# Second layer of a two-layer trunk: the first attention pair's projections, scores and sums ahead of the value projection, its transposes and value products behind it

## The chip, the cores and the metric

The kernel runs on one core of a Trainium2 chip. The metric is the device time of one execution in microseconds; before the change three runs had a median of 1221.72 us (1219.8 to 1224.15). The engines of the core are named as in the profile: PE multiplies matrices (PEld is its weight load), ACT applies functions and casts, DVE does elementwise work and scans, POOL is hardly used, and SP issues most of the transfers. Each engine works through its own queue in the order of the program and waits there on semaphores of the others.

## The reference

`x` is 512 x 1024 in float32. Layer 0 is left alone by this change. Layer 1 projects `x`, runs a gated recurrence (C) on one half of the channels and stick-breaking attention (D, 8 heads of 64) on the other, joins them with an output projection and a residual, and ends in a feed-forward block:

```
proj = x @ od_w_in[o]
xr, gr, qd, kd, vd = split_cols(proj, [LRU_WIDTH, LRU_WIDTH, HALF, HALF, HALF])
yc = rg_lru_branch(xr, gr, ...)
yd = stick_breaking_attention(qd, kd, vd)
mix = jnp.concatenate([yc, yd], axis=-1) @ od_w_out[o]
...
z = jnp.einsum('bqhd,bkhd->bhqk', q[:, q0:q1], k[:, :q1]).astype(jnp.float32) * scale
log_one_minus = jnp.where(mask, jax.nn.log_sigmoid(-z), 0.0)
suffix = lax.cumsum(log_one_minus, axis=3, reverse=True) - log_one_minus
log_w = jax.nn.log_sigmoid(z) + suffix
w = jnp.where(mask, jnp.exp(log_w), 0.0)
outs.append(jnp.einsum('bhqk,bkhd->bqhd', w.astype(v.dtype), v[:, :q1]))
```

The values `vd` are wanted only by the last of these lines.

## The kernel before

Matrices are multiplied in three passes: each float32 operand is split into a high part (a cast on ACT, L241 for weights, L247 elsewhere) and a low part (a subtraction on DVE, L242 and L248), and PE adds up high x high (L252), and the two mixed products (L253, L254). A projection of 128 output channels (`proj`, tile `pj`) is 24 matmuls over 512 columns; a weight chunk arrives by an SP transfer (L234) into one of two buffers `ws` and is split into one of five buffers `wh`, `wl`.

In layer 1 `griffin` does the recurrence: four channel blocks on ACT and DVE (L858 to L907), with four gate projections on PE beside them, and the split of its four results (L247, L248: `yh`, `yl`). Then `values` makes the 512 x 512 value matrix with four blocks of 24 matmuls (tile `pv`, copied out at L289). Then four calls of `sb_pair`, each for two heads:

- `qk_pair` projects q and k (24 matmuls each). q's bank is evacuated by ACT L723 and DVE L726, for each of two heads in turn; k's by ACT L730 and L731 and DVE L732 (`kz`), again for each head. ACT and DVE take turns on a bank.
- Five tiles of scores `z` (L933, L934, the mask L935), each followed by ACT L937 to L939 and DVE L940, L943 (a running sum, backwards) and L944, which leaves log weights `l`.
- Each tile is transposed on PE (L951, bank `pt` or `po`) and goes through exp into `pT` (ACT L957).
- 16 matmuls with the values (L964, tile `po`), and the split of the result.

Projections and values share two banks of the tag "g" in turn, so each new block of 24 matmuls has to wait until the one before the last has been evacuated.

What stands behind what on an engine is not set by the code's order alone: a scheduler orders the instructions by a priority that follows the order of the code, with weight splits pulled ahead by 600 places (`self.hp`). While one pair's ACT and DVE work runs, PE is given the next pair's projections; beside the fourth pair it has the recurrence's rows of the output projection (`out_rows`, 96 matmuls).

Of the kernel before, what the change touches and what calls it, by code (L numbers as in the profile page):

```python
# [11 lines left out]
AF = mybir.ActivationFunctionType  # L12
# [3 lines left out]
P = 128  # L16
# [28 lines left out]
S_GR, S_QD, S_KD, S_VD, S_WO1 = S_XR + 4, S_XR + 8, S_XR + 12, S_XR + 16, S_XR + 20  # L45
# [11 lines left out]
class Trunk:  # L57
# [853 lines left out]
        return ys  # L911


    def sb_pair(self, hp, v):
        nc = self.nc
        A = nc.scalar.activation
        q, k = self.qk_pair(S_QD + hp, S_KD + hp, self.kz)
        yh, yl = self.act("yh"), self.act("yl")
        po = self.bank("ho", "po")


        tiles = (((0, 3, 0),), ((1, 3, 0),), ((0, 2, 0), (0, 0, 384)), ((1, 2, 0), (1, 0, 384)), ((0, 1, 0), (1, 1, 256)))
        pT = self.t2k("pT", [P, 20 * P], tag="pT")
        at = ((15, -6), (1, 5))
        rev = lambda a: a[:, ::-1]
        for ti, parts in enumerate(tiles):
            tag = "zl"[ti % 2]
            l = self.t2k("l", tag=tag)
            ps = self.bank(("s", "s", "sc")[ti % 3], "z")
            for e, i, o in parts:  # L930
                n = (i + 1) * P
                c = slice(i * P, n)
                nc.tensor.matmul(ps[:, o:o + n], q[e][:, c], k[e][:, 0:n], start=True, stop=False)  # L933
                nc.tensor.matmul(ps[:, o:o + n], q[e][:, c], self.kz[e][:, 0:n], start=False, stop=False)  # L934
                nc.tensor.matmul(ps[:, o + i * P:o + n], self.identb, self.sbmask, start=False, stop=True)  # L935

            A(l, ps, AF.Abs)  # L937
            A(l, l, AF.Exp, scale=-1.0)
            A(l, l, AF.Ln, bias=self.one)  # L939
            nc.vector.scalar_tensor_tensor(l, ps, 0.0, l, ALU.max, ALU.add)  # L940
            for e, i, o in parts:
                r = rev(l[:, o:o + (i + 1) * P])
                nc.vector.tensor_tensor_scan(r, self.ones1[:, 0:(i + 1) * P], r, 0.0, ALU.mult, ALU.add)  # L943
            nc.vector.tensor_tensor(l, ps, l, ALU.subtract)  # L944
            pt = self.bank(("pt", "po")[ti % 2], "pt")
            for e, i, o in parts:
                b, step = at[e]
                for j in range(i + 1):

                    m = j if step > 0 else i - j  # L950
                    nc.tensor.transpose(pt[:, o + m * P:o + (m + 1) * P], l[:, o + j * P:o + (j + 1) * P], self.ident)  # L951
            for e, i, o in parts:
                b, step = at[e]
                lo = b + i + (0 if step > 0 else i * step)
                dst = bass.AP(tensor=pT.tensor, offset=pT.offset + lo * P,
                              ap=[pT.ap[0], [abs(step) * P, i + 1], [1, P]])
                A(dst, pt[:, o:o + (i + 1) * P].rearrange("p (j t) -> p j t", t=P), AF.Exp)  # L957
        cp = self.newest()

        for j in range(NTB):  # L960
            for e in range(2):
                h = 2 * hp + e
                x = (at[e][0] + at[e][1] * j + j) * P
                nc.tensor.matmul(po[64 * e:64 * e + 64, j * P:T], v[j][:, h * 64:h * 64 + 64], pT[:, x:x + T - j * P],  # L964
                                 start=j == 0, stop=j == NTB - 1)
                if j == 0 and e == 0:
                    self.behind(self.newest(), cp)
        self.put(po, yh, yl)
        return yh, yl

    def layer1(self, xr):
        self.qk4 = False

        self.kz = [self.t2k("kz", dt=F32R, tag="kz") for _ in range(2)]
        for e in range(2):
            self.nc.gpsimd.memset(self.kz[e][64 - 64 * e:P - 64 * e].bitcast(F32), 0.0)
        self.ones1 = self.t2k("ones", tag="one")
        self.nc.gpsimd.memset(self.ones1, 1.0)
        yc = self.griffin(xr)
        self.hp = 600  # L980
        v = self.values(S_VD)
        self.hp = 600
        yd = []
        for hp in range(4):
            yd.append(self.sb_pair(hp, v))
            if hp == 3:
                self.out_rows(yc, S_WO1)
        self.hp = 1
        return yd
# [123 lines left out]
```

## Time and profile before

| | us |
|---|---|
| median of three runs | 1221.72 |
| the profiled execution, its own time | 1221.14 |
| its span in the trace | 1219.3 |
| DVE busy in the span | 757.4 |
| ACT busy in the span | 518.6 |
| transfers, mean rate over the span | 105 GB/s |

In the span's time layer 1's value blocks run from 701 us to 723 us, the first pair's q and k from 723 to 736, and the four pairs from 736 to about 826. The list of groups gives for a line of the program the count, the busy time and the mean of one; the timeline gives start and length of each instruction, and in brackets how long its engine had been idle and who released it. Matmul lengths overlap, so the pace of PE is read from start to start.

### The profile page before, as it was taken

The page shows a single profiled execution, that of the slowest core. Times are in us where ns is not written, and L with a number is a line of the kernel's source. Part 1 is how long each engine was busy: PE and PEld are TensorE (multiplying, and loading weights), DVE is VectorE, ACT ScalarE, POOL GpSimd, SP SyncE. Part 2 cuts the span into 40 slices and gives each one's busy share as a digit, 9 for nine tenths or more (in the row PEclk, how much of TensorE's full clock was granted, in tenths as well). Part 3 has the DMA queues.
Part 4 walks back from the last instruction along what each step waited for, and adds up shares of the span by engine and source line. Part 5 has one row for each costly group of instructions (what it writes and reads, how often), then busy time and mean ns, then how long its engine had stood idle before and what let it go on. Part 6 is the DMA issues. An engine that isn't in the chain of part 4 may idle for free.

```text
span 1219.3 us, 15337 instructions
## 1 busy us (share of the span) xinstructions
PE 1196.5 (98%) x6063; PEld 970.6 (80%) x6063; DVE 757.4 (62%) x1141; ACT 518.6 (43%) x790; POOL 55.8 (5%) x80
## 2 busy tenths in 40 slices
PE   9999999999999999999999998999999999999997
PEld 6787777778888888878889786677988888888886
DVE  7638798769355634554368876887753644456346
ACT  7447568443233423332233667872332433333220
POOL 1000000001001000200000000000000100010001
PEclk9999999999999999999999999999999999999999
DMA  6421211233637432643324222112644643464321
GB/s 244 150 75 53 87 44 50 65 122 99 230 92 121 134 104 87 106 132 108 91 82 156 68 74 83 35 35 87 199 164 93 115 139 91 100 104 138 104 69 69
DMA packets 38727, 127.96 MB, mean 105 GB/s; under 512 B 4592, under 2 KB 6128, under 8 KB 38656
## 3 DMA queue, kind: packets, MB, share of 16 engines
q1 hardware_dynamic: 32496, 108.44, 28.0%
q0 software_dynamic: 4864, 16.81, 8.3%
q10 hardware_dynamic: 1296, 1.73, 0.4%
q8 instruction: 48, 0.79, 0.3%
q14 instruction: 23, 0.19, 0.1%
HBM read 124.84 MB, written 2.10 MB: 104 GB/s over the span
## 4 chain that ended last, share of the span: by engine, by line
PE 88%; DVE 4%; ACT 3%; DMA 2%; issue 1%; SPq 0%; DVEq 0%; ACTq 0%
PE pf L253 13%; PE pf L252 13%; PE pf L254 13%; PE pj L252 4%; PE pj L253 4%; PE pj L254 4%; PE po L254 4%; PE po L253 4%; PE po L252 4%; PE fa L252 2%; PE fa L254 2%; PE fa L253 2%; PE pv L253 2%; PE pv L252 2%; PE pv L254 2%; DMA wwal<-in_wst 1%
## 5 line engine op out<-in xcount | busy, mean ns | idle before, releaser
L241 ACT CAST wh<-ws 128x1024 fp32r<-128x1024 f32 x143 | 150.2, 1051 | 304.9 <-PE pf L253 121.8
L242 DVE TENSOR_TENSOR wl<-ws,wh 128x1024 fp32r<-128x1024 f32 x143 | 174.8, 1223 | 153.5 <-ACT wh L241 149.9
L252 PE MATMUL pf<-xh,wh 128*128 128x512 f32 x640 | 249.0, 389 | 0.0
L253 PE MATMUL pf<-xl,wh 128*128 128x512 f32 x640 | 249.0, 389 | 0.0
L254 PE MATMUL pf<-xh,wl 128*128 128x512 f32 x640 | 249.0, 389 | 0.0
L254 PEld LDWEIGHTS pf<-xh,wl 128*128 128x128 f32 x640 | 120.2, 188 | 25.0
L253 PEld LDWEIGHTS pf<-xl,wh 128*128 128x128 f32 x640 | 120.2, 188 | 24.9
L252 PEld LDWEIGHTS pf<-xh,wh 128*128 128x128 f32 x640 | 120.2, 188 | 24.7
L527 DVE TENSOR_TENSOR s<-s,pf 128x512 f32<-128x512 f32 x44 | 30.3, 688 | 148.0 <-PE pf L254 148.0
L252 PE MATMUL pj<-xh,wh 128*128 128x512 f32 x256 | 104.2, 407 | 2.1 <-DVE qk L726 2.1
L254 PE MATMUL pj<-xh,wl 128*128 128x512 f32 x256 | 104.0, 406 | 0.0
L253 PE MATMUL pj<-xl,wh 128*128 128x512 f32 x256 | 103.5, 404 | 0.2 <-DVE xl L248 0.2
L247 ACT CAST wh<-wwah 128x1024 fp32r<-128x1024 f32 x32 | 33.7, 1052 | 74.8 <-PE pf L253 63.3
L252 PEld LDWEIGHTS pj<-xh,wh 128*128 128x128 f32 x256 | 48.5, 190 | 13.6 <-DVE qk L726 2.6
L254 PEld LDWEIGHTS pj<-xh,wl 128*128 128x128 f32 x256 | 48.4, 189 | 10.3 <-issue 1.6
L253 PEld LDWEIGHTS pj<-xl,wh 128*128 128x128 f32 x256 | 48.5, 189 | 9.8 <-issue 1.0
L252 PE MATMUL po<-wh,yh 128*128 128x512 f32 x128 | 51.4, 401 | 0.0
L252 PE MATMUL fa<-wh,fm 128*128 128x512 f32 x128 | 50.0, 390 | 1.2 <-ACT wh L247 1.2
L253 PE MATMUL po<-wl,yh 128*128 128x512 f32 x128 | 51.0, 399 | 0.0
L254 PE MATMUL po<-wh,yl 128*128 128x512 f32 x128 | 50.9, 398 | 0.0
L248 DVE TENSOR_TENSOR wl<-wwah,wh 128x1024 fp32r<-128x1024 f32 x32 | 38.7, 1221 | 18.5 <-ACT wh L247 17.9
L254 PE MATMUL fa<-wh,fm 128*128 128x512 f32 x128 | 49.8, 389 | 0.0
(275 smaller groups left out, 2237.4 us busy)
## 6 DMA issues: line engine op xcount, KB each, us to landing
ws<-in_wst SPq DMA_DIRECT2D x165, 512.0 KB, 3.5
wwah<-in_wst POOLq DMA_DIRECT2D x24, 512.0 KB, 5.6
gb<-in_lnp SPq DMA_DIRECT2D x8, 512.0 KB, 5.1
wwah<-in_wst SPq DMA_DIRECT2D x8, 512.0 KB, 5.9
wwal<-in_wst SPq DMA_DIRECT2D x8, 512.0 KB, 6.8
wwal<-in_wst POOLq DMA_DIRECT2D x8, 512.0 KB, 6.1
ws<-in_wst SPq DMA_DIRECT2D x11, 256.0 KB, 5.2
xt<-in_xT SPq DMA_DIRECT2D x8, 256.0 KB, 5.2
```

What stands on the lines that cost most here:

```text
L241: nc.scalar.copy(hi, st)
L242: nc.vector.tensor_tensor(lo, st, hi.bitcast(F32), ALU.subtract)
L247: self.nc.scalar.copy(hi, dst)
L248: self.nc.vector.tensor_tensor(lo, dst, hi.bitcast(F32), ALU.subtract)
L252: mm(ps, ah, bh, start=first, stop=False, **kw)
L253: mm(ps, ah, bl, start=False, stop=False, **kw)
L254: mm(ps, al, bh, start=False, stop=last, **kw)
L527: nc.vector.tensor_tensor(h, h, pb, ALU.mult)
```

## The change

`sb_pair` gets an argument `between`. For the first pair it is a call of `values`, which is made after the five tiles' scores and sums; all five tiles of log weights are kept until then, and their transposes and exps follow. `v` is filled by that call and used by all four pairs. The other pairs run as before. The number of instructions on each engine stays as it was.

```
-    def sb_pair(self, hp, v):
+    def sb_pair(self, hp, v, between=None):
...
+        def turn(ti, parts, l):
+            pt = self.bank(("pt", "po")[ti % 2], "pt")
...
+                    nc.tensor.transpose(pt[:, o + m * P:o + (m + 1) * P], l[:, o + j * P:o + (j + 1) * P], self.ident)
...
+                A(dst, pt[:, o:o + (i + 1) * P].rearrange("p (j t) -> p j t", t=P), AF.Exp)
+
+        ls = []
         for ti, parts in enumerate(tiles):
...
             nc.vector.tensor_tensor(l, ps, l, ALU.subtract)
-            pt = self.bank(("pt", "po")[ti % 2], "pt")
...
+            if between:
+                ls.append((ti, parts, l))
+            else:
+                turn(ti, parts, l)
+        if between:
+            v = between()
+            for x in ls:
+                turn(*x)
         cp = self.newest()
...
         yc = self.griffin(xr)
         self.hp = 600
-        v = self.values(S_VD)
-        self.hp = 600
-        yd = []
+        yd, v = [], []
         for hp in range(4):
-            yd.append(self.sb_pair(hp, v))
+            yd.append(self.sb_pair(hp, v, (lambda: v.extend(self.values(S_VD)) or v) if hp == 0 else None))
```

The lines below `turn` have new numbers: in the changed kernel the scores are L950 to L952, their ACT work L954 to L956, their DVE work L957, L960 and L961, the transposes L934, the exps L940, and the products with the values L976. The names end in a running number, which differs between the two kernels for the same tile.

On PE, right behind the recurrence's last gate projection (`pj_5773`), there stood the first rows of the value block and three more blocks like it:

```order
L254 MATMUL pj_5773<-xh,wl_5770 128x512
L252 MATMUL pv_5849<-wh_5827,xh 128x512
L253 MATMUL pv_5849<-wl_5828,xh 128x512
L254 MATMUL pv_5849<-wh_5827,xl 128x512
```

Now q (`pj_5831`) and k (`pj_5866`) of the first pair stand there, and behind k's last matmul come these rows:

```order
L254 MATMUL pj_5866<-xh,wl_5863 128x512
L252 MATMUL pv_5996<-wh_5974,xh 128x512
L950 MATMUL z_5902<-qk_5823,qk_5821 128x512
L951 MATMUL z_5902<-kz_5503,qk_5821 128x512
L952 LDWEIGHTS identb
L952 MATMUL z_5902<-sbmask,identb 128x128
L950 MATMUL z_5924<-qk_5823,qk_5821 128x384
L950 MATMUL z_5913<-qk_5824,qk_5822 128x512
L951 MATMUL z_5924<-kz_5503,qk_5821 128x384
L951 MATMUL z_5913<-kz_5504,qk_5822 128x512
```

One matmul of the values is followed by the scores of three tiles; the other 95 of the values stand behind those (and around the last two tiles' scores). The first of them writes the "g" bank that q's projection had.

On DVE, at the end of the recurrence (its gate products L907, its last scan L895, and the low parts L248 of its results), there stood before:

```order
L907 TENSOR_TENSOR ig_5544<-ig_5544,ig_5545 128x512
L894 TENSOR_SCALAR w_5658<-w_5658 128x512
L907 TENSOR_TENSOR ig_5544<-ig_5544,ig_5545 128x512
L895 SCALAR_TENSOR_TENSOR ig_5544<-w_5658,ig_5544 128x512
L248 TENSOR_TENSOR yl_5803<-ig_5544,yh_5802 128x512
L907 TENSOR_TENSOR ig_5544<-ig_5544,ig_5545 128x512
L248 TENSOR_TENSOR yl_5808<-ig_5544,yh_5807 128x512
L907 TENSOR_TENSOR ig_5544<-ig_5544,ig_5545 128x512
L248 TENSOR_TENSOR yl_5813<-ig_5544,yh_5812 128x512
L248 TENSOR_TENSOR yl_5818<-ig_5544,yh_5817 128x512
```

Now the same place, one row further on, reads as follows, and only behind it come the four evacuations of q and k and the first scores' DVE work:

```order
L242 TENSOR_TENSOR wl_5993<-ws_5990,wh_5992 128x1024
L894 TENSOR_SCALAR w_5658<-w_5658 128x512
L907 TENSOR_TENSOR ig_5544<-ig_5544,ig_5545 128x512
L895 SCALAR_TENSOR_TENSOR ig_5544<-w_5658,ig_5544 128x512
L242 TENSOR_TENSOR wl_6150<-ws_6147,wh_6149 128x1024
L248 TENSOR_TENSOR yl_5803<-ig_5544,yh_5802 128x512
L907 TENSOR_TENSOR ig_5544<-ig_5544,ig_5545 128x512
L248 TENSOR_TENSOR yl_5808<-ig_5544,yh_5807 128x512
L907 TENSOR_TENSOR ig_5544<-ig_5544,ig_5545 128x512
L248 TENSOR_TENSOR yl_5813<-ig_5544,yh_5812 128x512
L726 SCALAR_TENSOR_TENSOR qk_5821<-pj_5831,qk_5821 64x512
L248 TENSOR_TENSOR yl_5818<-ig_5544,yh_5817 128x512
```

Two weight splits (the last of the values', and the second pair's q) have moved in among the rows of the recurrence, and q's first evacuation stands among the last of them; before, q's evacuations stood four weight splits behind the recurrence's last row.

The third place is on DVE where a pair's last scores meet the next pair's q. Before, for the first pair:

```order
L940 SCALAR_TENSOR_TENSOR l_6089<-z_6090,l_6089 128x512
L944 TENSOR_TENSOR l_6067<-z_6068,l_6067 128x512
L943 SCALAR_TENSOR_TENSOR l_6089<-ones_5507,l_6089 128x384
L943 SCALAR_TENSOR_TENSOR l_6089<-ones_5507,l_6089 128x128
L726 SCALAR_TENSOR_TENSOR qk_6143<-pj_6153,qk_6143 64x512
L944 TENSOR_TENSOR l_6089<-z_6090,l_6089 128x512
L242 TENSOR_TENSOR wl_6716<-ws_6713,wh_6715 128x1024
L940 SCALAR_TENSOR_TENSOR l_6111<-z_6112,l_6111 128x512
L726 SCALAR_TENSOR_TENSOR qk_6144<-pj_6153,qk_6144 64x512
```

Of the change, for the second pair:

```order
L957 SCALAR_TENSOR_TENSOR l_6279<-z_6280,l_6279 128x512
L961 TENSOR_TENSOR l_6257<-z_6258,l_6257 128x512
L960 SCALAR_TENSOR_TENSOR l_6279<-ones_5507,l_6279 128x384
L960 SCALAR_TENSOR_TENSOR l_6279<-ones_5507,l_6279 128x128
L726 SCALAR_TENSOR_TENSOR qk_6333<-pj_6343,qk_6333 64x512
L961 TENSOR_TENSOR l_6279<-z_6280,l_6279 128x512
L242 TENSOR_TENSOR wl_6784<-ws_6781,wh_6783 128x1024
L957 SCALAR_TENSOR_TENSOR l_6301<-z_6302,l_6301 128x512
L726 SCALAR_TENSOR_TENSOR qk_6334<-pj_6343,qk_6334 64x512
```

Row for row these are the same steps; the pattern of the first pair has moved to the second. The rows of the first pair's scores now stand alone on DVE, with no evacuation and no weight split among them.

More of the change, by code (lines that the diff above doesn't have):

```diff
@@ L925, in sb_pair @@
         rev = lambda a: a[:, ::-1]
+        def turn(ti, parts, l):
+            pt = self.bank(("pt", "po")[ti % 2], "pt")
+            for e, i, o in parts:
+                b, step = at[e]
+                for j in range(i + 1):
+                    m = j if step > 0 else i - j
+                    nc.tensor.transpose(pt[:, o + m * P:o + (m + 1) * P], l[:, o + j * P:o + (j + 1) * P], self.ident)
+            for e, i, o in parts:
+                b, step = at[e]
+                lo = b + i + (0 if step > 0 else i * step)
+                dst = bass.AP(tensor=pT.tensor, offset=pT.offset + lo * P,
+                              ap=[pT.ap[0], [abs(step) * P, i + 1], [1, P]])
+                A(dst, pt[:, o:o + (i + 1) * P].rearrange("p (j t) -> p j t", t=P), AF.Exp)
+        ls = []
         for ti, parts in enumerate(tiles):
@@ L944, in sb_pair @@
             nc.vector.tensor_tensor(l, ps, l, ALU.subtract)
-            pt = self.bank(("pt", "po")[ti % 2], "pt")
[L946 to L957, printed above, removed]
+            if between:
[6 more added lines that the diff above has]
+                turn(*x)
         cp = self.newest()
```

## The prediction

> **What bounds the kernel now.** I read the page first, then the busy time by stages, then PE's waits.
>
> ```profile
> PE 1196.5 (98%) x6063; PEld 970.6 (80%) x6063; DVE 757.4 (62%) x1141; ACT 518.6 (43%) x790; POOL 55.8 (5%) x80
> ```
>
> PE is busy 1196.5 of 1219.3 us. The change adds and removes no instruction, so only two things can move the time: PE's idle time, 22.8 us in all, and stretches in which its clock is lowered. The table of stages (columns: the stretch, its length, busy time of PE, PEld, DVE, ACT, POOL, then PE's granted clock, the transfers' share and rate) shows where they lie:
>
> ```profile
> 701.00:736.00 35.00, 35.00 (x154) 28.39 (x153) 25.55 (x37) 23.35 (x31) 0.00 (x0) 1.00 0.28 90
> 736.00:756.00 20.00, 15.73 (x81) 11.49 (x80) 16.10 (x23) 16.56 (x30) 0.00 (x0) 1.00 0.22 64
> 756.00:778.00 22.00, 21.38 (x108) 15.28 (x107) 17.09 (x26) 15.46 (x30) 0.00 (x0) 0.92 0.13 43
> 778.00:800.00 22.00, 20.08 (x109) 14.60 (x109) 18.15 (x25) 18.17 (x33) 0.00 (x0) 1.00 0.15 48
> 800.00:828.00 28.00, 26.59 (x145) 19.35 (x144) 21.79 (x32) 18.83 (x34) 0.00 (x0) 1.00 0.14 41
> 756.00:762.00 6.00, 6.00 (x24) 3.87 (x25) 2.95 (x6) 3.77 (x8) 0.00 (x0) 0.72 0.17 67
> ```
>
> The reader is to see three things. From 701 to 736 (values, then q and k of the first pair) PE never idles, and DVE is busy 25.55 of 35. In the four pairs PE idles 4.27, 0.62, 1.92 and 1.41 us, 8.22 in all. Right after the first pair the clock is 0.72 over 6 us, which costs 6 x 0.28 = 1.7 us. So the first pair loses 4.27 + 1.7 = 6.0 us. That is the most that the change could win there if nothing else happened. PE's list of waits says for what:
>
> ```profile
> PE pt L951 <- DVE l L944: 4.6, 9, 0.8
> PE pj L252 <- DVE qk L726: 2.1, 1, 2.1
> ```
>
> The 2.1 us are one wait: a new block of 24 matmuls needs the "g" bank of the q projection before it, and DVE evacuates that bank late because it is full of score work. Keep this wait in mind; the change makes another like it.
>
> **The change, step 1: when PE has done k.** q and k take the places of the first two value blocks, which ran without a gap:
>
> ```profile
> 701.05 0.39 PE L252 MATMUL pv<-wh,xh 128*128 128x512 f32 x1
> 711.78 0.39 PE L254 MATMUL pv<-wh,xl 128*128 128x512 f32 x1
> ```
>
> From the first to the last of 48 matmuls are 10.73 us, 0.228 each, so PE comes to the first matmul of the values at 712.0. Their weights hide as before: the transfers and splits of q and k stand where those of the values' first two chunks stood, and SP's queue keeps its order of issues by position.
>
> **Step 2: when DVE lets it go on.** That matmul writes q's bank, and needs both of q's DVE evacuations (L726). DVE's timeline at that time, without a gap:
>
> ```profile
> 703.66 1.22 DVE L242 TENSOR_TENSOR wl<-ws,wh 128x1024 fp32r<-128x1024 f32 x1
> 704.79 0.69 DVE L884 TENSOR_TENSOR dn<-dn,w 128x512 f32<-128x512 f32 x1
> ...
> 711.73 0.68 DVE L907 TENSOR_TENSOR ig<-ig,ig 128x512 f32<-128x512 f32 x1
> 712.34 0.41 DVE L894 TENSOR_SCALAR w<-w 128x512 f32<-128x512 f32 x1
> 712.67 0.68 DVE L907 TENSOR_TENSOR ig<-ig,ig 128x512 f32<-128x512 f32 x1
> 713.27 1.21 DVE L895 TENSOR_TENSOR_SCAN ig<-w,ig 128x512 f32<-128x512 f32 x1
> 714.41 0.66 DVE L248 TENSOR_TENSOR yl<-ig,yh 128x512 fp32r<-128x512 f32 x1
> 714.99 0.68 DVE L907 TENSOR_TENSOR ig<-ig,ig 128x512 f32<-128x512 f32 x1
> 715.59 0.68 DVE L248 TENSOR_TENSOR yl<-ig,yh 128x512 fp32r<-128x512 f32 x1
> ...
> 729.63 0.68 DVE L726 SCALAR_TENSOR_TENSOR qk<-pj,qk 64x512 fp32r<-64x512 f32 x1
> 730.98 0.69 DVE L726 SCALAR_TENSOR_TENSOR qk<-pj,qk 64x512 fp32r<-64x512 f32 x1 [0.66 <-ACT qk L723]
> ```
>
> Up to L907 at 711.73 the order has not changed in kind. From there I add up starts: L907 0.61, the values' last split 1.13 (703.66 to 704.79), L894 0.33, L907 0.60, the scan 1.14, the second pair's split 1.13, then L248, L907, L248, L907, L248 with 0.58, 0.60, 0.61, 0.60 and 0.61. That is 7.94 us, so q's first L726 starts at 719.67 and ends at 720.35. ACT's L723 for the second head takes its turn on the bank (0.59, below), and the second L726 runs from 721.0 to 721.7. **PE stands still from 712.0 to 721.7, 9.7 us**, with the other 95 matmuls of the values behind the waiting one. Bounds: without the two splits on the way 7.4; with one more 1.1 us step late 10.8. I take 9.7, since every step has a row.
>
> **Step 3: the scores.** Behind that matmul PE needs k's evacuations, and the bank's readers alternate:
>
> ```profile
> 730.35 0.59 ACT L723 ACTIVATE qk<-pj 64x512 fp32r<-64x512 f32 x1 [1.01 <-DVE qk L726]
> 735.08 0.58 ACT L730 CAST qk<-pj 64x512 fp32r<-64x512 f32 x1
> 738.27 0.69 DVE L732 TENSOR_TENSOR kz<-pj,qk 64x512 fp32r<-64x512 f32 x1 [1.24 <-ACT qk L731]
> ```
>
> From the start of L730 to the end of the second L732 are 3.88 us. ACT starts at 721.0, so the last `kz` is there at 724.9, and three tiles' scores end some 0.7 us later, at 725.6. PE's own work from 721.7 on is one matmul (0.23) and three tiles, by the starts of the same rows in the old first pair:
>
> ```profile
> 738.29 0.50 PE L933 MATMUL z<-qk,qk 128*128 128x512 f32 x1
> 738.63 0.40 PE L254 MATMUL pj<-xh,wl 128*128 128x512 f32 x1
> ...
> 739.32 0.40 PE L934 MATMUL z<-kz,qk 128*128 128x512 f32 x1
> ...
> 739.60 0.47 PE L254 MATMUL pj<-xh,wl 128*128 128x512 f32 x1
> ...
> 744.28 0.42 PE L933 MATMUL z<-qk,qk 128*128 128x384 f32 x1
> ...
> 745.06 0.48 PE L252 MATMUL pj<-xh,wh 128*128 128x512 f32 x1
> ```
>
> A tile of 512 takes 0.34 + 0.28 = 0.62, one of 384 and 128 takes 0.78, so two and one are 2.0. So 3.9 us hold 2.2 of work: **1.7 lost**, between 1.0 and 2.5.
>
> **Step 4: the clock.** After 9.7 us without work I expect a low clock as after the old first pair, at the price of that stretch: **1.7**, from 0.8 to 4.
>
> **Step 5: the first pair's sums are hidden.** From 725.6 on PE has 95 matmuls (21.7 us) and two tiles of scores. The chain of ACT and DVE for five tiles took 20 us in the old first pair, and is shorter now that DVE has no weight split among it. It costs PE nothing. What comes new is the end of the values: five tiles' transposes in a row on two banks, each bank waiting for its exp, and two weight casts in ACT's queue between these.
>
> ```profile
> 743.87 0.66 PE L951 MATMUL pt<-ident,l 128*128 128x128 f32 x4 [0.35 <-DVE l L944]
> 749.46 0.60 ACT L957 ACTIVATE pT<-pt 128x512 f32<-128x512 f32 x1 [1.91 <-PE pt L951]
> 751.29 0.64 ACT L957 ACTIVATE pT<-pt 128x384 f32<-128x384 f32 x2
> 734.00 1.05 ACT L241 CAST wh<-ws 128x1024 fp32r<-128x1024 f32 x1 [1.99 <-PE pj L253]
> ```
>
> ACT has 2 x 0.60 + 3 x 0.65 + 2 x 1.05 = 5.25, and starts 0.8 behind the first transposes: the products with the values can start after about 6.1. PE has 5 x 0.41 (743.87 to 744.28) and 12 projection matmuls, 4.8. **1.2 lost**, from 0.3 to 3 (above, if a cast also waits for its transfer; the page puts the landing of a chunk at 3.5 us).
>
> ```profile
> ws<-in_wst SPq DMA_DIRECT2D x165, 512.0 KB, 3.5
> ```
>
> **Step 6: the pairs behind.** Three pairs remain with a chain that PE has to cover. The second pair now has what the first had: its scores come when the third pair's q is under way, 10, 6, 12, 2 and 4 projection matmuls are spread between its tiles as before, and DVE's rows are the same. So I keep the loss of the old first pair (6.0) for the second, that of the old second for the third, and the last pair's. One ordinary pair's loss goes: **-1.9** (778 to 800). Bounds: -0.6 (756 to 778), and -6.0 if the loss was tied to the pair being first.
>
> **Sum.** 9.7 + 1.7 + 1.7 + 1.2 - 1.9 = +12.4 us. The profiled execution took 1221.14, 0.6 below the median: 1233.5.
>
> **The rivals.**
>
> Clock low for longer. In the quoted 6 us at 0.72 PE was fully busy, 6.00 of 6, and yet needed them to come back; here it is half busy up to 725.6. If the clock only comes back some 4 to 5 us of full work after that, steps 3 and 4 cost 2.4 more: 1236.
>
> [...]
>
> The big loss goes with the first pair. If the 2.1 us wait and the clock drop depended on something in the first pair that the second hasn't got, -6.0 stands in place of -1.9: 1229.4. With steps 2 to 5 at their lower ends also 1225. The equal rows on DVE speak against it.
>
> Faster: q's evacuations aren't late. Should DVE reach the second L726 by 711.3 (when PE, at 712.0, would just not wait), steps 2 to 4 fall away; with the first pair's 6.0 gone and the 1.2 paid that gives -4.8: 1216.3. DVE would have to be 10 us earlier in a queue that has no idle time from 703 to 717. If the second pair inherits the 6.0 even so: +1.2 - 1.9, 1220.4, no change that one could measure. That is also the case of a change that moves work but nothing on PE's path.
>
> **How the numbers follow.** Forecast 0.58; clock longer 0.17; second pair spared 0.14; neither stall nor gain 0.07; faster 0.04. A measurement of this kernel tells about 0.3% (3.7 us) from no change. Faster 0.04, within 0.07, slower 0.89. The range is 1226 to 1239: below, the spared pair with part of the lower bounds; above, the longer clock with step 5 at its upper end.
>
> **What would show it.** Right: PE idle from about 712 to 722, released by DVE L726, the longest of PE's waits; DVE's first L726 near 719.7; a clock below 1 between 718 and 731; no wait of PE within the value blocks; and then a wait near 2 us for L726 with a low clock in the second pair. Wrong: PE running through 712 to 722, or a second pair with less than 2 us of idle time.

## The result and the profile after

| | before | after |
|---|---|---|
| median, us | 1221.11 (6 runs, 1218.68 to 1224.15) | 1234.11 (6 runs, 1231.15 to 1235.82) |
| ratio | | 1.0103, 95% interval 1.0083 to 1.0123 |
| profiled execution, us | 1221.14 | 1235.82 |
| its span, us | 1219.3 | 1233.9 |

The changed kernel is 13.0 us slower. The page of the profiled execution shows PE as busy as before and a little longer:

```profile
PE 1200.5 (97%) x6063; PEld 972.5 (79%) x6063; DVE 757.7 (61%) x1141; ACT 518.0 (42%) x790; POOL 55.8 (5%) x80
```

PE was busy for 4.0 us more (1200.5 against 1196.5) with the same 6063 instructions, and idle for 33.4 us against 22.8. The table of stages below shows a lowered clock, at which the same matmuls take longer (those of the values start 0.43 us apart from 727.50 to 728.78, and 0.23 from 729.47 to 730.16, when the clock is back). PE's list of waits (total, times, longest) has a new first row:

```profile
PE pv L252 <- DVE qk L726: 9.9, 1, 9.9
PE pt L934 <- DVE l L961: 3.3, 7, 0.7
PE pj L252 <- DVE qk L726: 2.3, 2, 2.1
```

The first row is the predicted stall; the third holds a 2.1 us wait like the old first pair's, now in the second pair. Where the time goes is seen in the table of stages (stretch, length, busy time of PE, PEld, DVE, ACT and POOL, then PE's granted clock, the transfers' share and rate):

```profile
715.00:720.00 5.00, 0.00 (x0) 0.00 (x0) 5.00 (x8) 1.56 (x4) 0.00 (x0) 0.56 0.66 193
720.00:725.00 5.00, 2.41 (x6) 1.43 (x7) 3.28 (x6) 3.50 (x7) 0.00 (x0) 0.50 0.04 16
725.00:730.00 5.00, 5.00 (x17) 3.78 (x18) 3.52 (x5) 4.93 (x9) 0.00 (x0) 0.57 0.00 0
740.00:750.00 10.00, 10.00 (x46) 8.29 (x45) 1.44 (x2) 3.29 (x4) 0.00 (x0) 1.00 0.00 0
714.00:731.00 17.00, 8.41 (x28) 5.98 (x28) 13.80 (x21) 11.07 (x19) 0.00 (x0) 0.60 0.21 62
```

From 715 to 720 PE does nothing while DVE is busy 5.00 of 5. The clock is at half speed from inside the first of these rows (0.56) over the second (0.50) to inside the third (0.57). From 740 to 750 it is the other way round: PE is full, DVE does 1.44 of 10. The change moved DVE's score work to a place where it is well covered, and put q's evacuation where DVE had no room. DVE's timeline and PE's beside it:

```profile
712.28 0.68 DVE L907 TENSOR_TENSOR ig<-ig,ig 128x512 f32<-128x512 f32 x1
...
720.31 0.68 DVE L726 SCALAR_TENSOR_TENSOR qk<-pj,qk 64x512 fp32r<-64x512 f32 x1
721.02 0.69 DVE L248 TENSOR_TENSOR yl<-ig,yh 128x512 fp32r<-128x512 f32 x1
721.75 0.69 DVE L726 SCALAR_TENSOR_TENSOR qk<-pj,qk 64x512 fp32r<-64x512 f32 x1
```

```profile
722.59 0.76 PE L252 MATMUL pv<-wh,xh 128*128 128x512 f32 x1 [9.87 <-DVE qk L726]
...
726.93 0.78 PE L253 MATMUL pv<-wl,xh 128*128 128x512 f32 x1
...
729.21 0.42 PE L252 MATMUL pv<-wh,xh 128*128 128x512 f32 x1
...
751.23 1.03 PE L934 MATMUL pt<-ident,l 128*128 128x128 f32 x8
...
756.96 2.64 PE L976 MATMUL po<-pT,v 128*64 128x512 f32 x16
```

From L907 to the first L726 DVE needed 8.03 us. PE resumed when the second one had ended. The second pair then shows what the old first pair showed (a row of PE's timeline, then two stretches):

```profile
789.49 0.49 PE L252 MATMUL pj<-xh,wh 128*128 128x512 f32 x1 [2.09 <-DVE qk L726]
```

```profile
770.00:792.00 22.00, 17.80 (x88) 13.14 (x87) 18.12 (x26) 17.02 (x31) 0.00 (x0) 0.97 0.21 72
790.00:795.00 5.00, 5.00 (x19) 3.76 (x21) 2.72 (x5) 2.70 (x6) 0.00 (x0) 0.66 0.20 82
```

PE idles 4.20 us there (4.27 in the old first pair), and the low clock costs 5 x 0.34 = 1.7 us, the same price as before.

### The profile page after: what moved, and what is told of

Same layout as the page of the kernel before. It is cut to its first block, busy times and chain, and to the rows that moved or that the text cites. A ratio compares the mean times of both kernels' runs of the same rounds, so it can differ in the third digit from the quotient of the medians.

```text
span 1233.9 us, 15340 instructions
## 1 busy us (share of the span) xinstructions
PE 1200.5 (97%) x6063; PEld 972.5 (79%) x6063; DVE 757.7 (61%) x1141; ACT 518.0 (42%) x790; POOL 55.8 (5%) x80
## 4 chain that ended last, share of the span: by engine, by line
PE 84%; DVE 7%; DMA 4%; ACT 4%; issue 1%; SPq 0%; DVEq 0%; ACTq 0%
PE pf L253 13%; PE pf L252 13%; PE pf L254 13%; PE pj L252 4%; PE pj L253 4%; PE pj L254 4%; PE po L254 4%; PE po L252 4%; PE po L253 4%; PE fa L252 2%; PE fa L253 2%; PE fa L254 2%; DMA ws<-in_wst 2%; PE pv L253 2%; PE pv L252 2%; PE pv L254 2%
## 5 line engine op out<-in xcount | busy, mean ns | idle before, releaser
L252 PE MATMUL pf<-xh,wh 128*128 128x512 f32 x640 | 249.0, 389 | 0.0
L252 PEld LDWEIGHTS pf<-xh,wh 128*128 128x128 f32 x640 | 120.1, 188 | 24.8
L252 PE MATMUL pj<-xh,wh 128*128 128x512 f32 x256 | 104.3, 407 | 3.2 <-DVE qk L726 2.3
L247 ACT CAST wh<-wwah 128x1024 fp32r<-128x1024 f32 x32 | 33.7, 1053 | 73.9 <-PE pf L253 63.3
L252 PEld LDWEIGHTS pj<-xh,wh 128*128 128x128 f32 x256 | 48.5, 189 | 15.3 <-DVE qk L726 2.3
L252 PE MATMUL fa<-wh,fm 128*128 128x512 f32 x128 | 50.0, 391 | 2.2 <-ACT wh L247 2.2
L252 PE MATMUL po<-wh,yh 128*128 128x512 f32 x128 | 51.5, 403 | 0.0
L248 DVE TENSOR_TENSOR wl<-wwah,wh 128x1024 fp32r<-128x1024 f32 x32 | 38.8, 1221 | 18.5 <-ACT wh L247 17.9
L253 PE MATMUL fa<-wl,fm 128*128 128x512 f32 x128 | 49.8, 389 | 0.0
```

The costliest lines, as they stand in the source:

```text
L247: self.nc.scalar.copy(hi, dst)
L248: self.nc.vector.tensor_tensor(lo, dst, hi.bitcast(F32), ALU.subtract)
L252: mm(ps, ah, bh, start=first, stop=False, **kw)
L253: mm(ps, ah, bl, start=False, stop=False, **kw)
```

## Experiments

Each ratio is to executions of the kernel before that were taken together with the run (medians 1220.97, 1221.5 and 1220.47 us).

**Other banks for the values.** If PE waits for q's bank, it must go on when the value blocks use others.

```
-            ps = self.bank("g", "pv")
+            ps = self.bank(tags[tb], "pv")
...
-(lambda: v.extend(self.values(S_VD)) or v)
+(lambda: v.extend(self.values(S_VD, ("pt", "po", "g", "g"))) or v)
```

> The changed kernel, but the four value blocks take the PSUM banks of the tags pt, po, g, g in place of g four times, so the first two of them don't wait for q's and k's banks. Theory (PE stands for 9.9 us because its next matmul needs q's bank, which DVE evacuates late): PE now goes on behind k with 24 value matmuls and more, and stops only at the first scores or the third value block, some 2 to 4 us, until k's last evacuation near 725; the clock does not drop. The stall of 9.9 becomes 2 to 4 and the low clock's part of 3.2 goes: 1222 to 1227. The second pair still shows its wait near 2.1 us for DVE L726 with a clock below 1. Rival (PE waits for something else that is late at the same time, the bank is only named): a wait of 8 to 10 us stays in the first pair and the time stays at 1232 to 1236.

Measured: 1225.34 us (1224.07 to 1226.15), ratio to before 1.0033 (1.0020 to 1.0046). A row of PE's timeline, and two stretches:

```profile
721.02 0.68 PE L950 MATMUL z<-qk,qk 128*128 128x512 f32 x2 [2.45 <-ACT qk L731]
```

```profile
720.00:727.00 7.00, 5.98 (x22) 4.16 (x23) 3.16 (x5) 5.75 (x11) 0.00 (x0) 0.76 0.00 0
770.00:780.00 10.00, 6.20 (x33) 4.30 (x33) 9.62 (x15) 7.38 (x14) 0.00 (x0) 1.00 0.22 73
```

The stall of 9.87 is gone, and 2.45 us for k's evacuation are left in front of the scores. The theory holds, the rival falls: 8.8 us are won back. One part of the expectation failed: the clock dropped even after this short wait (0.76 over 7 us, 1.7 us). The second pair's loss is still there: 3.80 us idle in the ten shown, and its 2.1 us wait for DVE L726 stands in the list.

**Earlier evacuations.** The banks as in the changed kernel, but the first pair's evacuations of q and k have a higher priority by 600 places, on ACT and DVE, so that q's stand ahead of the recurrence's tail on DVE:

```
-        q, k = self.qk_pair(S_QD + hp, S_KD + hp, self.kz)
+        q, k = self.qk_pair(S_QD + hp, S_KD + hp, self.kz, ahead=0 if hp else 600)
...
+            with self.tc.high_priority(offset=ahead):
+                nc.scalar.mul(qs[e][d], qp[d], 0.125)
...
```

> The changed kernel, but the first pair's q and k evacuations (ACT and DVE) have a higher priority by 600 places: DVE's first one of q's bank stands ahead of the recurrence's last gate products and weight splits in place of behind them, and the banks stay as they are. Theory (the wait's length is the 8.0 us of older DVE work that stands ahead of q's evacuation): q's second evacuation ends by about 714, PE's wait there is 1 to 3 us in place of 9.9, PE has scores and values to do from there and its clock stays near 1; the DVE work that was passed comes later under the cover of 95 value matmuls. 1222 to 1227. Rival (what the recurrence's tail loses on DVE comes back on PE, since the last pair's output rows need its results): the wait is smaller but one near 8 us appears later; 1230 to 1236.

Measured: 1224.83 us (1223.32 to 1228.25), ratio 1.0038 (1.0023 to 1.0053). The evacuation L726 is L727 in this kernel. DVE's timeline, PE's, and a stretch:

```profile
713.12 0.68 DVE L727 SCALAR_TENSOR_TENSOR qk<-pj,qk 64x512 fp32r<-64x512 f32 x1
```

```profile
716.27 0.77 PE L252 MATMUL pv<-wh,xh 128*128 128x512 f32 x1 [2.79 <-DVE qk L727]
```

```profile
714.00:721.00 7.00, 4.73 (x18) 3.80 (x19) 6.88 (x9) 6.49 (x10) 0.00 (x0) 0.76 0.23 75
```

With q's first evacuation at 713.12 in place of 720.31 the wait is 2.79 in place of 9.87. So most of the stall was the DVE work queued ahead of L726. The recurrence's tail, which now comes later, is paid for nowhere: no wait near 8 us appears. Again the clock dropped (0.76 over 7 us), against the expectation.

**q and k ahead, the scores not.** Only the projections are moved; scores, sums and transposes stand behind the values as before the change:

```
+        if between:
+            v = between()
         ls = []
         for ti, parts in enumerate(tiles):
...
-            if between:
-                ls.append((ti, parts, l))
-            else:
-                turn(ti, parts, l)
-        if between:
-            v = between()
-            for x in ls:
-                turn(*x)
+            turn(ti, parts, l)
```

> One part of the change alone: q and k of the first pair come ahead of the values, but the scores, sums and transposes come behind all four value blocks, as before the change. Theory (the stall comes from q's bank, which any block behind q and k needs, and not from the scores): PE waits 9 to 10 us for DVE L726 behind k as in the changed kernel, and then runs through 95 value matmuls; the first pair's chain stands behind the values, covered by the second pair's projections as before the change, so its loss of 6.0 stays in the first pair: 1230 to 1236. Rival (it is the scores, put so near to k, that hold PE up): no wait above 3 us behind k, and 1219 to 1224.

Measured: 1228.62 us (1227.88 to 1229.19), ratio 1.0060 (1.0044 to 1.0076), below the range that the theory gave. PE's timeline and two stretches:

```profile
721.46 0.76 PE L252 MATMUL pv<-wh,xh 128*128 128x512 f32 x1 [9.88 <-DVE qk L726]
```

```profile
714.00:728.00 14.00, 6.54 (x20) 5.22 (x21) 8.62 (x12) 4.71 (x8) 0.00 (x0) 0.63 0.24 75
740.00:840.00 100.00, 94.74 (x493) 71.14 (x492) 77.57 (x107) 74.12 (x129) 0.00 (x0) 1.00 0.21 64
```

The stall is the same to 0.01 us without any score near it, so the scores have no part in it. The theory holds for the stall. What the theory had wrong is the rest: it left the first pair's loss of 6.0 in place, but no pair has the 2.1 us wait any more, and the clock is 1.00 over all four pairs. PE idles 5.26 us there; before it was 8.22, and 1.7 of low clock. The sum closes: 9.88 for the stall, 2.3 for value matmuls at half clock from 721.46 to 726, and -4.7 in the pairs give +7.5; the medians differ by 7.65.

**Work in the stall.** Forty matmuls that nobody reads keep PE busy, to take the low clock away and leave the stall:

```
+        if between:
+            fill = self.bank("pt", "fill")
+            for _ in range(40):
+                nc.tensor.matmul(fill, self.xh[:, 0, 0:P], self.xh[:, 1, :], start=True, stop=True)
```

> The changed kernel with 40 matmuls added behind k's projection, 128 x 512 each, from operands that are there into a bank of another tag; nobody reads what they give. They take about 9.1 us of the 9.9 in which PE waits, so that PE is busy there and only the low clock is taken away. Theory (the low clock behind the stall costs about 1.1 us among the value matmuls and a part of the 2.1 among the scores, the stall itself costs 9.9): PE still comes to the first value matmul's successor at the same time, 722 to 723; the granted clock stays at 0.95 or more from 712 to 735, and the time is 1 to 3 us below the changed kernel's 1234.1, so 1231 to 1233. Rival (the clock costs nothing of its own, the scores wait for the evacuations anyway): no change, 1233.5 to 1235. A second rival (the added work delays the evacuations or the first scores): above 1236.

Measured: 1232.79 us (1231.73 to 1235.06), ratio 1.0099 (1.0083 to 1.0114): not to be told from the changed kernel. The stages, and PE's waits among the scores (L954 and L955 here):

```profile
715.00:720.00 5.00, 5.00 (x24) 3.98 (x22) 4.95 (x8) 1.78 (x3) 0.00 (x0) 1.00 0.43 147
721.00:731.00 10.00, 8.81 (x27) 6.50 (x28) 5.50 (x8) 6.71 (x12) 0.00 (x0) 0.66 0.00 1
```

```profile
721.31 0.50 PE L954 MATMUL z<-qk,qk 128*128 128x512 f32 x1 [1.08 <-ACT qk L731]
722.12 0.47 PE L955 MATMUL z<-kz,qk 128*128 128x512 f32 x1 [0.31 <-DVE kz L732]
723.23 0.79 PE L954 MATMUL z<-qk,qk 128*128 128x512 f32 x1 [0.57 <-ACT qk L731]
```

The work filled the stall, and the clock was 1.00 up to 720. It then dropped all the same, behind pauses of 1.08 and 0.31 us among the scores and within a third of 0.57. So this run did not do what it was made for: the time lies in the theory's range, but the clock did not stay at 0.95, and the price of the low clock by itself is not measured. It does show that a low clock comes here without the long stall, too. Among the scores and values, half speed lasted 6.8 us here and 6.7 in the changed kernel (722.59 to 729.25), so its price was paid in both.

**Both cures.** q and k ahead without the scores, and the values in the banks pt, po, g, g (the edits of the first and the third run together).

> Both cures at once: as in the run with q and k alone ahead (scores, sums and transposes behind the value blocks), and the value blocks take the banks pt, po, g, g. Theory (the whole loss of the change is the bank; and four pairs whose scores find q and k evacuated long before lose less, 100.00 - 94.74 = 5.26 us of PE time from 740 to 840 there, against 8.22 and 1.7 of low clock before): no wait above 1 us for DVE L726 at all, since the third value block is reached at about 712.3 + 10.9 = 723.2 and q's second evacuation ends near 722; the clock stays at 1.00 from 700 to 840; the time is 1221 - 4.7 = 1216, between 1215 and 1218. Rival (the pairs' gain hangs on the pause that the stall gave DVE and ACT to work off their queues): the wait of 2.1 and the low clock come back in one pair, 1219 to 1222.

Measured: 1216.14 us (1215.29 to 1217.96), ratio 0.9959 (0.9947 to 0.9972): faster than both kernels, and where the theory put it. Its stages, then PE's timeline at the first pair's scores; below them the stage of before:

```profile
700.00:740.00 40.00, 40.00 (x181) 32.61 (x180) 28.43 (x41) 28.87 (x42) 0.00 (x0) 1.00 0.26 79
740.00:840.00 100.00, 94.70 (x491) 71.31 (x489) 80.87 (x117) 68.46 (x119) 0.99 (x1) 1.00 0.20 64
```

```profile
734.29 0.23 PE L954 MATMUL z<-sbmask,identb 128*128 128x128 bf16 x1
734.34 0.48 PE L252 MATMUL pj<-xh,wh 128*128 128x512 f32 x1
```

```profile
736.00:840.00 104.00, 95.78 (x492) 70.61 (x492) 80.18 (x112) 72.35 (x128) 0.00 (x0) 0.98 0.19 57
```

PE does not idle from 700 to 740, and the pairs lose 5.30 us although no pause has given DVE and ACT time to catch up; so the gain did not hang on the stall, and the rival falls. The cure has little room: in this profile the third value block, the first in a bank g, starts at 721.59, 1.0 us after the second evacuation of that bank has ended on DVE (719.92 and 0.69 more). The two rows of the timeline show a possible reason for the pairs' gain: the second pair's first projection matmul comes behind the scores, so that all 48 of them cover the first pair's chain. Before the change 14 of them (9, 2 and 3) stood ahead of or among the first three tiles' scores, to bridge k's evacuation, and 34 were left. That this cover is the reason is read from the traces; it was not varied by itself.

**Values in two halves.** q, k, two value blocks in pt and po, the scores and sums, two value blocks in g, the transposes. The value projection becomes a generator here that stops behind each block:

```
+        if between:
+            v = []
+            blocks = self.values_by_block(S_VD, v, ("pt", "po", "g", "g"))
+            next(blocks)
+            next(blocks)
...
-            v = between()
+            list(blocks)
...
```

> q and k of the first pair, two value blocks in the banks pt and po, the scores and sums, the other two value blocks in g, and the transposes. Theory (the stall goes when 48 matmuls, 10.9 us, stand between k and the scores): no wait above 1 us before the transposes and a clock of 1.00 there; the second pair has its 2.1 wait and its low clock, since it is spread as in the changed kernel: 1234.1 - 9.9 - 3.2 = 1221, between 1219.5 and 1222.5, no change from before. Rival (with the stall the second pair's loss goes too): 1215 to 1217. Second rival (the scores between two blocks wait as in the run with other banks, 2.5 us and a low clock): 1224 to 1226.

Measured: 1223.43 us (1221.49 to 1225.32), ratio 1.0014 (1.0005 to 1.0023), 1 us above the theory's range. PE's waits (q's evacuation on DVE is L731 in this kernel) and two stretches:

```profile
PE pj L252 <- DVE qk L731: 2.1, 1, 2.1
...
PE z L960 <- DVE l L971: 1.0, 1, 1.0
```

```profile
720.00:740.00 20.00, 18.16 (x92) 14.10 (x90) 14.91 (x21) 14.95 (x26) 0.00 (x0) 1.00 0.04 9
768.00:785.00 17.00, 13.21 (x59) 9.35 (x59) 12.94 (x19) 11.67 (x23) 0.00 (x0) 0.80 0.22 63
```

The stall is gone and the second pair's 2.1 us wait is there, as the theory said; the first rival falls. The second is half right: the scores do wait, but the clock stays at 1.00 there. Two things cost more than I had put: 1.84 us of small waits among the scores, and a low clock that lasted 6.8 us (17 x 0.20 x 2, at half speed) behind the same 2.1 us wait that elsewhere brings 3.4.

**Evacuations earlier, without the change.** The kernel before, with the evacuations of the later pairs pulled ahead:

```
-        q, k = self.qk_pair(S_QD + hp, S_KD + hp, self.kz)
+        q, k = self.qk_pair(S_QD + hp, S_KD + hp, self.kz, ahead=150 if hp else 0)
```

> The kernel before, with the q and k evacuations of the second to the fourth pair at a priority higher by 150 places, so that DVE takes the second pair's first L727 ten rows earlier. Theory (the 2.1 us wait and the low clock behind it, 3.8 us in all, come from q's late evacuation on DVE alone, whichever pair it is): both go, 1221 - 3.8 = 1217, between 1216 and 1219. Rival (the score chain that is passed by then ends later and PE waits for that in its place, with the same low clock): 1220 to 1223.

Measured: 1218.10 us (1217.12 to 1220.36), ratio 0.9978 (0.9968 to 0.9989). A row of PE's waits (the transposes are L953 here, q's evacuation L727), and the four pairs:

```profile
PE pt L953 <- DVE l L946: 6.2, 11, 1.9
```

```profile
736.00:840.00 104.00, 96.94 (x506) 74.12 (x505) 82.54 (x116) 74.10 (x129) 0.28 (x1) 1.00 0.19 61
```

The wait for L727 is gone, and in this profile the low clock with it; the time is 3.4 us lower by the medians, where the theory had 3.8. This confirms that the wait came from the late evacuation. A part of the rival is true too: the transposes wait 6.2 us for the score chains in place of 4.6, so that PE idles 7.06 us in place of 8.22, and it is the clock (1.00) that brings the larger part.

**Halves and earlier evacuations.** The edits of the last two runs together.

> The run with values split in two halves, and the evacuations of the second to fourth pair at a priority higher by 150 places, too. Theory: neither the first pair's stall nor the 2.1 us wait of the second is left, nor a low clock: 1221 - 3.8 - 1 (three pairs with a chain in place of four) = 1216, between 1214.5 and 1218. Rival (the passed score chain becomes the wait): 1220 to 1223.

Measured: 1218.01 us (1216.95 to 1219.76), ratio 0.9973 (0.9963 to 0.9982), at the upper edge of the theory's range. The stretch of the first pair's scores still loses:

```profile
700.00:740.00 40.00, 38.15 (x178) 30.48 (x177) 34.83 (x53) 30.64 (x46) 0.00 (x0) 1.00 0.16 48
```

The wait of 2.1 us and the low clock are gone, as the theory said, so the rival falls. Those 1.85 us of waits among the scores are what bringing the scores ahead costs here. By the medians it lies 1.9 above the run with both cures, which leaves the scores behind the values; the intervals of the two ratios overlap a little.

**A control.** The run with both cures, and the evacuations of the later pairs pulled ahead.

> The run with q and k ahead and the value blocks in pt, po, g, g, and on top of it the evacuations of the second to fourth pair at a priority higher by 150 places. A control: if those evacuations helped the kernel before only by the one 2.1 us wait and its low clock, which this order of work hasn't got, they bring nothing here: 1216, between 1215 and 1217.5, with the list of PE's waits led by the transposes' (DVE l) at about 4 us as before. Rival (early evacuations help every pair by themselves): 1212 to 1214.5. Second rival (the passed score chains end later): 1217.5 to 1220.

Measured: 1218.16 us (12 runs, 1215.66 to 1222.34), ratio 0.9985 (0.9975 to 0.9994), slower than without the priorities. The profiled execution was the fastest of the twelve, so its span says little. Its waits and its pairs say more:

```profile
PE pt L936 <- DVE l L965: 4.8, 9, 0.8
PE pt L936 <- ACT l L960: 1.8, 1, 1.8
```

```profile
740.00:840.00 100.00, 93.11 (x489) 70.06 (x490) 80.74 (x115) 68.10 (x118) 0.99 (x1) 1.00 0.20 62
```

By the ratios to before it is some 3 us slower than the run with both cures, and the intervals do not meet. PE idles 6.89 us in the pairs against 5.30, 1.6 more, for the transposes: the early evacuations pass the score chain for which the next transpose waits. The second rival holds for this half of the loss; the other half the profile does not show. Where there was a 2.1 us wait to win, the early evacuations paid; here there is nothing to win.

## Why the prediction was right

| step | predicted, us | in the trace, us |
|---|---|---|
| 1: PE done with k | 712.0 | 712.56 (last matmul 712.33) |
| 2: the stall | 9.7 | 10.03 (712.56 to 722.59; 9.87 in the list of waits) |
| 3 and 4: scores, low clock | 1.7 + 1.7 | 3.2, all of it low clock |
| 5: transposes in a row | 1.2 | 0.9 |
| 6: one ordinary pair's loss | -1.9 | -1.55 |
| sum | +12.4 | +12.6 |
| median | 1233.5 | 1234.11 |

**Step 2** was right in place, cause and size: the row of 712.28 to 720.31 is 8.03 us where I had added up 7.94 from rows of before. Three runs stand behind the cause. Another bank takes the stall away; an earlier evacuation shrinks it to 2.79; moving the scores back does not touch it.

**Steps 3 and 4** were right in sum and wrong in both parts, so that the fit of their sum is luck. PE needed from 722.59 to 726.93, 4.34 us, for 2.23 of work (2.1 lost), and to 729.21 for five matmuls of 0.228 (1.1 lost). The timeline names no wait among these scores, where step 3 had 1.7 us of waits for k's evacuations. All of the 3.2 goes with half speed: the five matmuls took 2.28 us for 1.14 of work, twice as long, and at that pace 2.23 us of work are 4.46 (an estimate), which already fills the 4.34. Step 4 had 1.7 for the clock, about half of that. At this clock (0.50 from 720 to 725) the scores ran so slowly, as I read it, that no wait was left between them; in this stretch the two terms cover each other and do not add up. The run with the filled stall shows the other side: there the scores begin at full clock, and the pauses are 1.08, 0.31 and 0.57, 1.96 us in sum.

**The rival of a longer low clock** was nearer to the trace than the forecast, and wrong in the price. The stretch from 725 to 730 at 0.57 holds 4.3 us of half speed, so the clock was back at 729.3. That is 3.7 us after 725.6, the time from which the rival wanted 4 to 5, an estimate of mine that no run shows. While PE had work, half speed lasted 6.7 us, twice the 3.4 of the old first pair. But the rival added its 2.4 us to waits that did not come: steps 3 and 4 cost 3.2, where it had 5.8.

**Step 5**: from 751.23 to 756.96 are 5.73 us with 4.8 of work. The list names no wait for the exps or the casts there, and PE idles only 0.12 us from 750 to 758, so the cause of the 0.9 is not shown. Within the value blocks PE had no wait, as said.

**Step 6**: the second pair lost 4.20 and 1.7, the old first pair 4.27 and 1.7. The three later pairs' idle time (0.62, 1.92 and 1.41, 3.95 in sum) became 2.4 in two. I had taken the inheritance from equal rows on DVE. The trace shows more of why: an ordinary pair has the 16 products of the pair ahead to do during its own score chain, but the products of the first pair now run from 756.96 on, well ahead of the second pair's scores (770.14 in the timeline). The old first pair had none to do either. This, too, is read and not tried. The rival of a spared second pair fell for this order of work; that the loss can go altogether is shown by the two runs with q and k alone ahead, where no pair has it.

The profiled executions differ by 14.7 us, the steps make 12.6. Of the rest 0.55 lies ahead of step 1 (711.78 has become 712.33), and 1.0 in the waits of the feed-forward block (PE fa L252 for ACT wh L247; 2.2 in the list against 1.2), which are 0.6 in the run with other banks and not in the list of the one with the filled stall; so they vary between executions. The 0.55 is less than a wait of 0.90 us at 12.8 us (PE L252 for ACT xh L247), in layer 0, that the profile before does not have. What is left, 0.5, I did not trace. The medians differ by 13.0.

## What to carry to other kernels

When a block of matmuls is moved, look at which bank it will hold and who has to empty that bank at its new place. The cost is read from the queue of the emptying engine, summed row by row, not from PE. Here the idea to hide the first pair was sound, but its loss moved on to the second pair; what paid was to bring only the projections ahead and to give the first two blocks of work behind them other banks, so that the projections' banks were wanted 10.9 us later (48 matmuls of 0.228) and the scores came more than 20 us later.

## What the runs showed of the hardware

The low clock came in pieces of one length here. In steps of half a microsecond around the first pair, both kernels and four of the runs (other banks, the first pair's evacuations earlier, q and k alone ahead, the filled stall) show a granted clock of 1.00 or 0.50, and values between only in the steps in which it changes. So the time at half speed is 2 x (1 - granted clock) x stretch: 3.4 us behind the old first pair (6 us at 0.72), 3.4 in the runs with other banks and with the first pair's evacuations earlier (7 us at 0.76), 6.8 with the filled stall (10 us at 0.66), 10.4 with q and k alone ahead (14 us at 0.63), 13.6 in the changed kernel (17 us at 0.60): about one, two, three and four times 3.4. PE did not have to stand still for as long as that: the 3.4 us came with waits of 2.1 us in the kernel before, and of 2.45 and 2.79 us in the two runs, and with the filled stall the clock fell behind pauses of 1.08 and 0.31 us and within a third of 0.57.

The length of a wait alone does not decide it in these traces. In layer 0, which the change leaves alone, all eleven traces have the same wait of 1.8 us. Ten of them have a piece of half speed behind it, the trace of the control has none: the mean granted clock of its profiled execution is 0.998, that of the ten 0.991 to 0.997 (0.997 with both cures, whose clock is 1.00 from 700 to 1200 as the control's is). PE's timeline and the stretch behind it, first before, then the control:

```profile
236.66 0.50 PE L762 MATMUL s<-qk 128*128 128x128 f32 x2 [1.81 <-DVE qk L731]
237.00:243.00 6.00, 5.77 (x23) 4.37 (x23) 3.23 (x11) 2.83 (x11) 0.00 (x0) 0.72 0.18 73
```

```profile
236.68 0.50 PE L764 MATMUL s<-qk 128*128 128x128 f32 x2 [1.82 <-DVE qk L733]
237.00:243.00 6.00, 5.77 (x32) 4.29 (x31) 4.63 (x14) 3.74 (x13) 0.00 (x0) 1.00 0.20 76
```

A wait of 1.9 us for a transpose in the kernel before with earlier evacuations left the clock at 1.00, too (1.00 from 736 to 840). So one wait near 2 us cost about 1.7 us of clock or nothing, and in the run with halved values, where half speed lasted 6.8 us, nearly twice that. The mean granted clock of 25 executions of the kernel before lies between 0.992 and 0.998, while one piece makes 0.0014 (an estimate: half of 3.4 us, over 1219.3). A low clock that one profile shows, or doesn't, is therefore no sure property of the order of work. What decides whether the clock falls behind such a wait is not shown.
